# Moving the wait loop of a merge branch behind gate blocks, and the gate steps to the head of a background queue

## The chip, the cores and the metric

One core of a Trainium2 chip runs the kernel. The metric is the device time of one execution in microseconds (us). The kernel is given as three timed executions and one profiled one. TensorE is called PE, its weight loads PEld, VectorE DVE, ScalarE ACT, GpSimd POOL, SyncE SP.

## The reference

Two layers over a sequence of 512 tokens of width 1024, all in fp32. Each layer mixes three token mixers (retention, gated linear attention, softmax attention with forget gates) through gates of their own, then runs a gated feed-forward with a convolution over three tokens.

```python
def hybrid_layer(x, c_act, ...):
    mod = c_act @ w_ada + b_ada
    shift1, scale1, gate1, shift2, scale2, gate2 = jnp.split(mod, 6, axis=-1)
    h = modulate(rms_norm(x, norm1_g), shift1, scale1)
    (rq, rk, rv, rg, gq, gk, gv, glr, gg, fq, fk, fv, ff) = jnp.split(h @ w_in, split_points, axis=-1)
...
    ret = jax.nn.silu(rg) * ret          # retention of rq, rk, rv, group norm
...
    log_a = jax.nn.log_sigmoid((glr @ w_gla_a2 + b_gla_a).astype(F32)) / GLA_TAU
...
    gla_o = jax.nn.silu(gg) * gla_o      # gated linear attention of gq, gk, gv, log_a
    fox_o = forgetting_attention(rms_norm(heads(fq, FOX_D), q_norm_g),
                                 rms_norm(heads(fk, FOX_D), k_norm_g),
                                 heads(fv, FOX_D), ff + b_fox_f).reshape(b, s, BRANCH_W)
    branches = jnp.stack([ret, gla_o, fox_o], axis=2).astype(h.dtype)
    y_br = jnp.einsum('bsnw,nwd->bsnd', branches, w_br)
    gates = jax.nn.sigmoid(h @ w_mg + b_mg).reshape(b, s, N_BRANCH, D_MODEL)
    mixed = jnp.sum(gates * y_br, axis=2) @ w_o
    x = x + (gate1[:, None, :] * mixed).astype(x.dtype)
...
    u, g = jnp.split(h2 @ w_up, 2, axis=-1)
    u = causal_dwconv(u, w_conv, b_conv)
    y = (jax.nn.silu(u) * g) @ w_down
```

## The kernel before

The activations stay transposed in SBUF as 128x512 tiles (`slot`), eight for a width of 1024. A product in fp32 is three matmuls: a tile is split into a high part that ACT casts (`hi`) and a low part that DVE subtracts (`lo`), and `mm3` (L293 to L295) multiplies high by high, high by low and low by high. Weights come as units of 128x1024 from the DRAM tensor `wall`, in the order in which they are used. For each unit SP issues the transfer, ACT casts (L173, `wh`) and DVE subtracts (L182, `wl`). For the pair groups (below) POOL also issues transfers that add one unit onto another (L165).

A layer runs a foreground stream on PE: the head group, the remaining key/query blocks, a token group (`tok_group`, gla keys and the small columns of both gates, L694 to L696), two blocks `gq`, two pair groups (`pair_group`: seven products `prod` of 2 x 12 = 24 matmuls, L644 to L648; the first gives fox and gla values, the second ret values and the ret gate), the blocks `rq`, `rk`, `gg`, the merge, the output block and the feed-forward. A column block `col_block` is 24 matmuls.

Everything small runs as **background items**, Python generators on `queue`. An item is a chain of steps. A step marked "p" issues PE work, needs PSUM banks of the pool `psa` (three banks, NA) and can have conditions on earlier results; a step marked "e" issues what ACT, DVE and POOL do with it. `tick()` takes at most one item from the queue if the counter `cool` is 0 (the second number of a queue entry is the new `cool`), then advances every active item by one "e" step, evacuates the foreground blocks that are done, and advances by one "p" step. A column block ticks in the middle and at the end, a pair product once. The order of each engine is thus fixed by the ticks when the program is built; at run time each engine takes its instructions in that order.

The items that matter: `qk_norm` (eight, L541 to L561: square, cast, two matmuls `qn` with a tile of ones, then L551 to L554 on ACT), `gates_item` (transposes `smT`, L726, L731 to L733, L737 to L740 with a scan over tokens, transposes `cumc` L744, then POOL's DMAs `cumd` and `cumb` L747 and L750 which spread the sums over the partitions), `la_item` (two: `la`, `laS`, `lan`, the log-decays), `fox_item` (sixteen: scores `fs` L802, softmax, transposes `fT` L818, values `fo` L828), `kv_item` (states of gla, L871), `ret_item` (sixteen: `rs` L941, `ro` L953, then L962 to L972 for the norm), `gla_item` (`go` L919, L927 to L933), and `head_out` (L895 to L908, transposes `oT` L902, L531 and L532 for the split).

The merge runs over three branches, `order = (2, 0, 1)`: fox, ret, gla. A branch has four rounds, each of two gate blocks (gate logits of two column blocks) and 24 matmuls with the branch's result (`fb` tiles for fox, `ob` for ret and gla). Ahead of a branch's first gate block a loop ticks until the branch's last head is ready, without foreground work between the ticks. From the merge on in layer 0, every second tick also does an ada step on DVE (L203, a product of 128x1024).

Of the kernel before, what the change touches and what calls it, by code (L numbers as in the profile page):

```python
# [10 lines left out]
AF = mybir.ActivationFunctionType  # L11
# [15 lines left out]
NH = 4  # L27
HD = 128
DFF = 2816
KD = D // 128  # L30
# [20 lines left out]
NC = _o  # L51


H0 = slice(0, S // 2)
H1 = slice(S // 2, S)

# [30 lines left out]
def tile_hybrid_layers(ctx: ExitStack, tc: tile.TileContext, xT, cvec, wall, wada, par, a2, cst, tabs, out):  # L87
# [14 lines left out]
    def slot(nm, dt=F32):  # L102
        return slots.tile([128, S], dt, tag="slot", name=nm)
# [39 lines left out]
    def dbg(*a):  # L143
        if DBG:
            print(*a, tickcount[0], "unit", cur[0])
# [99 lines left out]
    queue = []  # L245
# [19 lines left out]
    def tick(n=1, fl=True):  # L265
        for g in active:
            g[2] = False
        if cool[0] > 0:
            cool[0] -= 1
        if queue and len(active) < 8 and cool[0] == 0:  # L270
            it, cool[0] = queue.pop(0)
            active.append([it, next(it), False])
        advance("e")
        if fl:
            flush()
        advance("p")
        if ada_on[0] and tickcount[0] % 2 == 1:
            ada_step()
        tickcount[0] += 1
        if DBG:  # L280
            print("T", tickcount[0], len(active), len(queue), live[0], cur[0], [g[0].__name__ for g in active])

    tickcount = [0]
    cool = [0]
# [17 lines left out]
    def ahead():  # L302
        prep_to(cur[0] + depth[0])
        dma_to(cur[0] + depth[0] + far[0], far[0] > 1)
# [230 lines left out]
    def layer(l, nm, h):  # L535
# [43 lines left out]
        A.preload_act_table_set("natural_log_exp_and_others")  # L579
        for i, o in enumerate(banks):  # L580
            qk_evac(i)(o)
        cool[0] = 8
        ahead()
        free(NA)

# [30 lines left out]
            tt[k, 1], tt[k, 2] = (ah, al, 0), (ah, al, 256)  # L616
            tt[k, 3], tt[k, 4] = (bh, bl, 0), (bh, bl, 256)

        def pair_group(done):
            flush()  # L620
            while live[0] > NA - 1:
                tick()
            q = {}
            for k in range(4):
                q[k, 11], q[k, 12] = (*h[k], 0), (*h[k], 256)
                q[k, 21], q[k, 22] = (*h[k + 4], 0), (*h[k + 4], 256)
            bA, bB = [bm(), bm()], [bm(), bm()]
            o11, o12, o21, o22 = ([slot("pr"), slot("pr")] for _ in range(4))

            def prod(banks, key, first, evac):  # L630
                us = []
                for t in range(2):
                    flush()
                    prep_lo(cur[0] + 3 - t)
                    prep_hi(cur[0] + 4 - t)
                    dma_to(cur[0] + 10, True)
                    if not t:
                        us = [unit(), unit()]
                    for k in range(4):
                        ah, al, o = q[k, key] if key > 4 else tt[k, key]  # L640
                        ts = slice(o + t * 128, o + t * 128 + 128)
                        wh, wl = us[k // 2]
                        ws = slice((k % 2) * S, (k % 2) * S + S)
                        T.matmul(banks[t], lhsT=ah[:, ts], rhs=wh[:, ws], start=first and k == 0, stop=False,  # L644
                                 skip_group_check=True)
                        T.matmul(banks[t], lhsT=ah[:, ts], rhs=wl[:, ws], start=False, stop=False,  # L646
                                 skip_group_check=True)
                        T.matmul(banks[t], lhsT=al[:, ts], rhs=wh[:, ws], start=False, stop=k == 3,  # L648
                                 skip_group_check=True)
                        if k == 1 and not t:  # L650
                            tick()
                    pend.append(lambda t=t: evac(t))

            prod(bA, 11, True, lambda t: A.copy(o11[t], bA[t]))
            prod(bB, 1, True, lambda t: A.copy(o22[t], bB[t]))
            while live[0] > NA - 1:
                tick()
            bC = [bm(), ba()]

            def e11(t):  # L660
                V.tensor_tensor(o11[t], o11[t], bC[t], op=ALU.add)
                if t:
                    free()

            prod(bC, 21, True, e11)
            prod(bA, 2, False, lambda t: A.copy(o12[t], bA[t]))
            prod(bA, 3, False, lambda t: V.scalar_tensor_tensor(out=o22[t], in0=bA[t], scalar=-1.0, in1=o22[t],
                                                                op0=ALU.mult, op1=ALU.subtract))
            prod(bB, 22, False, lambda t: V.tensor_tensor(o12[t], o12[t], bB[t], op=ALU.add))

            def e21(t):
                A.activation(o21[t], bA[t], AF.Copy, scale=-1.0)
                if t:
                    done(o11 + o12, o21 + o22)

            prod(bA, 4, False, e21)
# [27 lines left out]
        def gk_evac(b, o):  # L704
            if b == 0:
                R["gk"] = [slot("gk"), slot("gk")]
                R["sml"] = sm_p.tile([128, NB, 20], F32, tag="sml", name="sml")
            A.copy(R["gk"][b // 2][:, (b % 2) * 256:(b % 2) * 256 + 256], o[:, 0:256])
            V.tensor_copy(R["sml"][:, b, :], o[:, 256:276])  # L709
            if b == NB - 1:  # L710
                queue.append((gates_item(), 1))
                queue.append((la_item(0), 1))
                queue.append((la_item(1), 1))
                for hh in range(NH):
                    for ib in range(NB):
                        queue.append((fox_item(hh, ib), 1 + ib // 2))
# [281 lines left out]
                R["rv", b] = v[b]  # L998
                R["rg"].append(t)

        pair_group(fg_done)
        R["cos"], R["sin"] = slot("cos"), slot("sin")
        Q.dma_start(out=R["cos"], in_=tabs[0])
        Q.dma_start(out=R["sin"], in_=tabs[1])
        pair_group(r_done)
        tt.clear()
        far[0] = 1
        for i in range(4):
# [18 lines left out]
        for bi, br in enumerate(order):  # L1027
            dbg("mg", bi, br)
            if bi == 2:
# [3 lines left out]
                for _ in range(200):  # L1033
                    if not (queue or active):
                        break
                    tick()
            while ("br", br, NH - 1) not in R:
                tick()
            dbg("mg start", bi, br)
            for pr in range(KD // 2):  # L1040
                gts = {}

                def sg_evac(i, j, gts=gts):
                    def f(o):
                        g = slot("mg")
                        A.activation(g, o, AF.Tanh, scale=0.5, bias=der[l][:, i * 8 + j:i * 8 + j + 1])  # L1046
                        gts[j] = g
                    return f

                for j in (2 * pr, 2 * pr + 1):  # L1050
                    col_block(h, sg_evac(br, j))
                ahead()
                wh, wl = unit()
                for jj in range(2):
# [186 lines left out]
def _layout(inputs):  # L1241
# [17 lines left out]
    def put(tiles):  # L1259
        units.append(np.concatenate(list(tiles), axis=1))  # L1260

    for l in range(L):
# [35 lines left out]
        for br in (2, 0, 1):  # L1298
            wg = f["w_mg"][l][:, br * D:(br + 1) * D]
            wb = f["w_br"][l, br]  # L1300
            for pr in range(KD // 2):
                put(blk(wg, 2 * pr))
                put(blk(wg, 2 * pr + 1))
                put(list(blk(wb, 2 * pr)) + list(blk(wb, 2 * pr + 1)))
        cols(f["w_o"][l])
        wu = f["w_up"][l][:, :DFF]
# [93 lines left out]
```

## Time and profile before

| | before |
|---|---|
| three timed executions, median (us) | 1839.98 (1839.25 to 1844.28) |
| profiled execution (us) | 1841.36 |
| its span (us) | 1839.6 |
| PE busy (us, share of the span) | 1797.5 (98%) |
| DVE busy | 1068.0 (58%) |
| ACT busy | 724.1 (39%) |
| POOL busy | 126.4 (7%) |

The span reaches from the first instruction of the profile to the last; 1.8 us of the profiled execution lie around it. A busy share is the time in which an engine has an instruction under way. Matmuls overlap, so two of them that start 0.23 us apart are each listed with 0.4 us; the distance of the starts tells what one costs.

### The profile page before, as it was taken

The page shows a single profiled execution, that of the slowest core. Times are in us where ns is not written, and L with a number is a line of the kernel's source. Part 1 is how long each engine was busy: PE and PEld are TensorE (multiplying, and loading weights), DVE is VectorE, ACT ScalarE, POOL GpSimd, SP SyncE. Part 2 cuts the span into 40 slices and gives each one's busy share as a digit, 9 for nine tenths or more (in the row PEclk, how much of TensorE's full clock was granted, in tenths as well). Part 3 has the DMA queues.
Part 4 walks back from the last instruction along what each step waited for, and adds up shares of the span by engine and source line. Part 5 has one row for each costly group of instructions (what it writes and reads, how often), then busy time and mean ns, then how long its engine had stood idle before and what let it go on. Part 6 is the DMA issues. An engine that isn't in the chain of part 4 may idle for free.

```text
span 1839.6 us, 22717 instructions
## 1 busy us (share of the span) xinstructions
PE 1797.5 (98%) x8895; PEld 1497.6 (81%) x8895; DVE 1068.0 (58%) x1643; ACT 724.1 (39%) x1196; POOL 126.4 (7%) x152
## 2 busy tenths in 40 slices
PE   9999899999999999999999999999999999999999
PEld 6877686888889888888897777778888898888887
DVE  7867765675665776763246777644634566444321
ACT  3567442342333443332136664424323244333220
POOL 3122110010000000000001221100100000000000
PEclk9999898999999999999999999999999999999999
DMA  9487133346552465553323771312332233222131
GB/s 356 126 195 202 46 118 112 126 142 224 195 168 82 155 228 192 183 204 128 109 76 101 189 208 42 126 64 64 123 116 92 71 102 115 92 94 102 43 126 50
DMA packets 72519, 243.11 MB, mean 132 GB/s; under 512 B 8232, under 2 KB 8658, under 8 KB 72412
## 3 DMA queue, kind: packets, MB, share of 16 engines
q1 hardware_dynamic: 66444, 220.67, 35.5%
q0 software_dynamic: 5968, 20.99, 5.8%
q8 instruction: 70, 1.15, 0.3%
q14 instruction: 37, 0.30, 0.0%
HBM read 237.41 MB, written 4.21 MB: 131 GB/s over the span
## 4 chain that ended last, share of the span: by engine, by line
PE 80%; DVE 8%; ACT 4%; DMA 4%; issue 3%; POOL 1%; SPq 0%; ACTq 0%; DVEq 0%; POOLq 0%
PE bm L293 22%; PE bm L295 22%; PE bm L294 22%; PE bm L426 4%; PE ga L426 4%; DMA wr<-wall 3%; ACT wh L173 2%; DVE wl L182 2%; PE rs L941 1%; PE ro L953 1%; DVE fl L808 1%; PE bm L644 1%; PE bm L646 1%; PE bm L648 1%; DVE fst L809 1%
## 5 line engine op out<-in xcount | busy, mean ns | idle before, releaser
L182 DVE TENSOR_TENSOR wl<-wr,wh 128x1024 fp32r<-128x1024 f32 x326 | 396.9, 1222 | 301.8 <-ACT wh L173 301.6
L293 PE MATMUL bm<-hhi,wh 128*128 128x512 f32 x1232 | 500.5, 406 | 2.2 <-DVE sml L709 2.2
L295 PE MATMUL bm<-hhi,wl 128*128 128x512 f32 x1232 | 484.0, 393 | 0.0
L294 PE MATMUL bm<-hlo,wh 128*128 128x512 f32 x1232 | 483.7, 393 | 0.0
L173 ACT CAST wh<-wr 128x1024 fp32r<-128x1024 f32 x326 | 339.1, 1049 | 327.0 <-PE bm L294 201.6
L293 PEld LDWEIGHTS bm<-hhi,wh 128*128 128x128 f32 x1232 | 234.2, 190 | 56.3 <-issue 5.0
L294 PEld LDWEIGHTS bm<-hlo,wh 128*128 128x128 f32 x1232 | 233.8, 190 | 52.5 <-issue 3.7
L295 PEld LDWEIGHTS bm<-hhi,wl 128*128 128x128 f32 x1232 | 233.5, 190 | 50.2
L293 PE MATMUL bm<-fah,wh 128*128 128x512 f32 (+1 forms) x374 | 141.0, 377 | 0.0
L295 PE MATMUL bm<-fah,wl 128*128 128x512 f32 (+1 forms) x374 | 140.8, 377 | 0.0
L294 PE MATMUL bm<-fal,wh 128*128 128x512 f32 (+1 forms) x374 | 140.8, 377 | 0.0
L203 DVE SCALAR_TENSOR_TENSOR ar<-ar,cact 128x1024 f32<-128x1024 f32 x80 | 97.5, 1219 | 0.0
L1083 DVE SCALAR_TENSOR_TENSOR x<-bm,mod,x 128x512 f32<-128x512 f32 (+1 forms) x39 | 25.5, 654 | 103.1 <-PE bm L295 103.0
L295 PEld LDWEIGHTS bm<-fah,wl 128*128 128x128 f32 x374 | 70.4, 188 | 13.0
L293 PEld LDWEIGHTS bm<-fah,wh 128*128 128x128 f32 x374 | 70.4, 188 | 12.9
L294 PEld LDWEIGHTS bm<-fal,wh 128*128 128x128 f32 x374 | 70.4, 188 | 12.8
L1046 ACT ACTIVATE mg<-bm,der 128x512 f32<-128x512 f32 x48 | 33.1, 689 | 95.9 <-PE bm L295 95.9
L1120 ACT ACTIVATE fu<-fu 128x512 f32<-128x512 f32 x44 | 27.9, 635 | 103.0 <-DVE fu L1118 103.0
L1121 DVE TENSOR_TENSOR fu<-fu,bm 128x512 f32<-128x512 f32 x42 | 28.9, 688 | 64.8 <-PE bm L295 53.4
L332 ACT ACTIVATE sq<-x 128x512 f32<-128x512 f32 (+1 forms) x35 | 18.8, 547 | 104.1 <-DVE x L1083 102.9
L293 PE MATMUL bm<-mxh,wh 128*128 128x256 f32 (+1 forms) x176 | 58.6, 333 | 0.0
L295 PE MATMUL bm<-mxh,wl 128*128 128x256 f32 (+1 forms) x176 | 58.3, 331 | 0.0
(259 smaller groups left out, 2733.7 us busy)
## 6 DMA issues: line engine op xcount, KB each, us to landing
wr<-wall SPq DMA_DIRECT2D x302, 512.0 KB, 3.8
ar<-wada SPq DMA_DIRECT2D x80, 512.0 KB, 4.3
wr<-wall POOLq DMA_DIRECT2D x32, 512.0 KB, 7.7
ad<-wada SPq DMA_DIRECT2D x32, 256.0 KB, 6.1
x<-xT SPq DMA_DIRECT2D x16, 256.0 KB, 5.3
cumb<-cumd POOLq DMA_DIRECT2D x8, 256.0 KB, 5.4
dec<-tabs SPq DMA_DIRECT2D x8, 256.0 KB, 2.7
x<-xs SPq DMA_DIRECT2D x8, 256.0 KB, 5.4
```

Of the source, the lines that this page charges most:

```text
L173: A.copy(hi, raw[plan[i][1]])
L182: V.tensor_tensor(lo, raw[plan[i][1]], hi.bitcast(F32), op=ALU.subtract)
L203: V.scalar_tensor_tensor(out=r, in0=r, scalar=1.0, in1=cact, op0=ALU.mult, op1=ALU.mult, accum_out=mod[l][:, b:b + 1])
L293: T.matmul(o, lhsT=wh, rhs=ah, start=first, stop=False)
L294: T.matmul(o, lhsT=wh, rhs=al, start=False, stop=False)
L295: T.matmul(o, lhsT=wl, rhs=ah, start=False, stop=last)
L332: A.activation(t[:, ts], x[k][:, ts], AF.Square)
L426: T.matmul(banks[f % GB][:, ts], lhsT=got[f // 8][wi][:, (f % 8) * 128:(f % 8) * 128 + 128], rhs=h[kc][hi][:, ts], start=kc == 0 and hf != ...
L1046: A.activation(g, o, AF.Tanh, scale=0.5, bias=der[l][:, i * 8 + j:i * 8 + j + 1])
L1083: V.scalar_tensor_tensor(out=x[j][:, ts], in0=o[:, ts], scalar=mod[l][:, sec * 8 + j:sec * 8 + j + 1], in1=x[j][:, ts], op0=ALU.mult, op1= ...
L1120: A.activation(t, t, AF.Silu)
L1121: V.tensor_tensor(t, t, pg, op=ALU.mult)
```

## The change

Four edits. **One**: in the merge, the gate blocks are grouped by the tables MG0 (first branch: four blocks, none, two, two) and MG1 (the others: two each), and the loop that waits for the branch's last head stands behind the round's gate blocks, ahead of its product with the branch's result. The host packs the weights in the same order. **Two**: `gates_item` and the two `la_item` go to the head of the queue instead of its end, each with a `cool` of 2. **Three**: the first `cool` is 12 in layer 1, 8 in layer 0 as before. **Four**: a pair group is told how many ticks each of its seven products has; in the second pair the last three have two.

```diff
@@ -51,6 +51,8 @@
 NC = _o
 
 
+MG0 = ((0, 1, 2, 3), (), (4, 5), (6, 7))
+MG1 = ((0, 1), (2, 3), (4, 5), (6, 7))
 H0 = slice(0, S // 2)
 H1 = slice(S // 2, S)
 
@@ -579,7 +581,7 @@
         A.preload_act_table_set("natural_log_exp_and_others")
         for i, o in enumerate(banks):
             qk_evac(i)(o)
-        cool[0] = 8
+        cool[0] = 12 if l else 8
         ahead()
         free(NA)
 
@@ -616,7 +618,7 @@
             tt[k, 1], tt[k, 2] = (ah, al, 0), (ah, al, 256)
             tt[k, 3], tt[k, 4] = (bh, bl, 0), (bh, bl, 256)
 
-        def pair_group(done):
+        def pair_group(done, nts):
             flush()
             while live[0] > NA - 1:
                 tick()
@@ -629,6 +631,7 @@
 
             def prod(banks, key, first, evac):
                 us = []
+                nt = nts.pop(0)
                 for t in range(2):
                     flush()
                     prep_lo(cur[0] + 3 - t)
@@ -647,7 +650,7 @@
                                  skip_group_check=True)
                         T.matmul(banks[t], lhsT=al[:, ts], rhs=wh[:, ws], start=False, stop=k == 3,
                                  skip_group_check=True)
-                        if k == 1 and not t:
+                        if k == 1 and t < nt:
                             tick()
                     pend.append(lambda t=t: evac(t))
 
@@ -708,9 +711,7 @@
             A.copy(R["gk"][b // 2][:, (b % 2) * 256:(b % 2) * 256 + 256], o[:, 0:256])
             V.tensor_copy(R["sml"][:, b, :], o[:, 256:276])
             if b == NB - 1:
-                queue.append((gates_item(), 1))
-                queue.append((la_item(0), 1))
-                queue.append((la_item(1), 1))
+                queue[0:0] = [(gates_item(), 2), (la_item(0), 2), (la_item(1), 2)]
                 for hh in range(NH):
                     for ib in range(NB):
                         queue.append((fox_item(hh, ib), 1 + ib // 2))
@@ -998,11 +999,11 @@
                 R["rv", b] = v[b]
                 R["rg"].append(t)
 
-        pair_group(fg_done)
+        pair_group(fg_done, [1] * 7)
         R["cos"], R["sin"] = slot("cos"), slot("sin")
         Q.dma_start(out=R["cos"], in_=tabs[0])
         Q.dma_start(out=R["sin"], in_=tabs[1])
-        pair_group(r_done)
+        pair_group(r_done, [1] * 4 + [2] * 3)
         tt.clear()
         far[0] = 1
         for i in range(4):
@@ -1034,21 +1035,20 @@
                     if not (queue or active):
                         break
                     tick()
-            while ("br", br, NH - 1) not in R:
-                tick()
-            dbg("mg start", bi, br)
-            for pr in range(KD // 2):
-                gts = {}
-
-                def sg_evac(i, j, gts=gts):
-                    def f(o):
-                        g = slot("mg")
-                        A.activation(g, o, AF.Tanh, scale=0.5, bias=der[l][:, i * 8 + j:i * 8 + j + 1])
-                        gts[j] = g
-                    return f
-
-                for j in (2 * pr, 2 * pr + 1):
+            gts = {}
+
+            def sg_evac(i, j, gts=gts):
+                def f(o):
+                    g = slot("mg")
+                    A.activation(g, o, AF.Tanh, scale=0.5, bias=der[l][:, i * 8 + j:i * 8 + j + 1])
+                    gts[j] = g
+                return f
+
+            for pr, gs in enumerate(MG0 if bi == 0 else MG1):
+                for j in gs:
                     col_block(h, sg_evac(br, j))
+                while ("br", br, NH - 1) not in R:
+                    tick()
                 ahead()
                 wh, wl = unit()
                 for jj in range(2):
@@ -1298,9 +1298,9 @@
         for br in (2, 0, 1):
             wg = f["w_mg"][l][:, br * D:(br + 1) * D]
             wb = f["w_br"][l, br]
-            for pr in range(KD // 2):
-                put(blk(wg, 2 * pr))
-                put(blk(wg, 2 * pr + 1))
+            for pr, gs in enumerate(MG0 if br == 2 else MG1):
+                for j in gs:
+                    put(blk(wg, j))
                 put(list(blk(wb, 2 * pr)) + list(blk(wb, 2 * pr + 1)))
         cols(f["w_o"][l])
         wu = f["w_up"][l][:, :DFF]
```

In the changed file these lines stand one to three lower, so L533 there is L531 before, L963 is L962, L997 is L996, L903 is L902.

PE in the first merge branch of layer 0. `fo`, `fT` and `fs` are the fox steps, `kv` the gla states, `rs` the ret scores, `bm<-hhi` the gate blocks, `bm<-fbh` the products with the fox result. Before, between the last column block and the first gate block:

```order
L295 MATMUL bm<-hhi,wl 128x512
L828 MATMUL fo<-fpT,pr 128x128 x4
L818 MATMUL fT<-cst,fl 128x128 x3
L802 MATMUL fs<-qk 128x512
L828 MATMUL fo<-fpT,pr 128x128
L818 MATMUL fT<-cst,fl 128x128 x3
L828 MATMUL fo<-fpT,pr 128x128 x2
L871 MATMUL kv<-pr,lae 64x128 x8
L828 MATMUL fo<-fpT,pr 128x128 x3
L818 MATMUL fT<-cst,fl 128x128 x4
L871 MATMUL kv<-pr,lae 64x128 x8
L828 MATMUL fo<-fpT,pr 128x128 x4
```

After, the last half of the fourth gate block and the first product with the fox result:

```order
L297 MATMUL bm<-hhi,wl 128x512
L872 MATMUL kv<-pr,lae 64x128 x8
L942 MATMUL rs<-rq,rk 128x512
L295 MATMUL bm<-hhi,wh 128x512
...
L297 MATMUL bm<-hhi,wl 128x512
L942 MATMUL rs<-rq,rk 128x384
L295 MATMUL bm<-fbh,wh 128x512
```

The fox steps and the `kv` steps have moved in between half gate blocks.

ACT at the end of the second pair group of layer 0. L672 and L675 are the same evacuation of a pair product, L996 and L997 the tanh of the ret gate. Before:

```order
L672 ACTIVATE pr<-bm 128x512
L996 ACT_TABLE_LOAD
L996 ACTIVATE rg<-pr 128x512 x4
L173 CAST wh<-wr 128x1024
L770 ACTIVATE lae<-la 128x512
L771 ACTIVATE lae<-lae 128x512
L772 ACT_TABLE_LOAD
```

After:

```order
L544 ACTIVATE qsq<-qk 128x512
L675 ACTIVATE pr<-bm 128x512
L997 ACT_TABLE_LOAD
L997 ACTIVATE rg<-pr 128x512 x4
L553 ACT_TABLE_LOAD
L553 ACTIVATE qy<-qn,cst 128x512
L554 ACTIVATE qv<-qn,cst 128x512
L555 ACT_TABLE_LOAD
L555 ACTIVATE qy<-qy 128x512
L556 ACTIVATE qsq<-qy 128x512
L530 CAST qsh<-qsq 128x512
```

The log-decay steps (L770 to L772) have left this place, and steps of the key/query norm have come to it.

PE at the start of the second merge branch (ret) of layer 0. `oT` are the transposes of `head_out` (`ros` for ret, `gos` for gla), `ro` and `go` the values of ret and gla. Before, between the last product with the fox result and the first gate block:

```order
L295 MATMUL bm<-fbh,wl 128x512
L902 MATMUL oT<-cst,gos 128x128 x4
L919 MATMUL go<-st,gq 64x128 x8
L902 MATMUL oT<-cst,ros 128x128 x4
L902 MATMUL oT<-cst,gos 128x128 x4
L919 MATMUL go<-st,gq 64x128 x8
L293 MATMUL bm<-hhi,wh 128x512
```

After, between the second gate block and the first product with the ret result:

```order
L297 MATMUL bm<-hhi,wl 128x512
L903 MATMUL oT<-cst,ros 128x128 x4
L954 MATMUL ro<-pr,rP 128x128 x4
L920 MATMUL go<-st,gq 64x128 x8
L903 MATMUL oT<-cst,gos 128x128 x4
L920 MATMUL go<-st,gq 64x128 x8
L903 MATMUL oT<-cst,ros 128x128 x4
L903 MATMUL oT<-cst,gos 128x128 x4
L920 MATMUL go<-st,gq 64x128 x8
L295 MATMUL bm<-obh,wh 128x512
```

The short loop has moved behind two gate blocks, and it holds eight pieces instead of five.

## Rows read from the trace of the kernel before

**Rows 1.** The page's first section: busy time, share and instructions of each engine.

```profile
PE 1797.5 (98%) x8895; PEld 1497.6 (81%) x8895; DVE 1068.0 (58%) x1643; ACT 724.1 (39%) x1196; POOL 126.4 (7%) x152
```

**Rows 2.** Waits of PE: line, releaser, us in total, times, longest us.

```profile
PE qn L547 <- ACT qsh L528: 4.1, 1, 4.1
...
PE cumc L744 <- DVE cum L740: 3.3, 1, 3.3
PE bm L293 <- DVE sml L709: 2.2, 1, 2.2
```

**Rows 3.** Timeline of PE, layer 1, column block: start us, duration, instruction.

```profile
1191.13 0.39 PE L295 MATMUL bm<-hhi,wl 128*128 128x512 f32 x1
1191.36 0.60 PE L828 MATMUL fo<-fpT,pr 128*128 128x128 f32 x4
1191.89 0.67 PE L871 MATMUL kv<-pr,lae 64*64 64x128 f32 x16
```

**Rows 4.** Windows: length; busy PE, PEld, DVE, ACT, POOL; PE clock; DMA share; GB/s.

```profile
84.00:89.44 5.44, 5.44 (x24) 4.52 (x25) 5.06 (x13) 4.26 (x8) 0.09 (x1) 1.00 0.01 2
...
181.41:215.50 34.09, 26.99 (x104) 21.53 (x103) 22.53 (x37) 18.86 (x30) 5.67 (x7) 0.80 0.21 62
1066.38:1111.45 45.07, 41.21 (x185) 32.80 (x184) 32.25 (x46) 26.77 (x43) 5.77 (x8) 0.96 0.67 202
278.81:302.58 23.77, 19.48 (x119) 13.44 (x118) 14.48 (x33) 7.70 (x15) 0.00 (x0) 0.71 0.25 83
1195.35:1207.78 12.43, 10.62 (x81) 7.63 (x80) 7.31 (x17) 3.57 (x5) 0.00 (x0) 0.86 0.14 44
386.22:390.84 4.62, 3.67 (x46) 2.92 (x44) 3.31 (x8) 2.96 (x12) 0.85 (x1) 1.00 0.02 4
990.61:1004.26 13.65, 9.51 (x30) 7.06 (x28) 10.86 (x22) 9.01 (x18) 1.28 (x1) 0.75 0.00 0
...
996.40:1004.26 7.86, 7.86 (x26) 6.21 (x24) 5.79 (x12) 5.53 (x13) 1.28 (x1) 0.68 0.00 0
```

**Rows 5.** Timeline of ACT, layer 0, end of the second pair group.

```profile
180.63 0.57 ACT L672 ACTIVATE pr<-bm 128x512 f32<-128x512 f32 x1
181.22 1.28 ACT L996 ACT_TABLE_LOAD   x1
182.51 2.19 ACT L996 ACTIVATE rg<-pr 128x512 f32<-128x512 f32 x4
184.61 1.04 ACT L173 CAST wh<-wr 128x1024 fp32r<-128x1024 f32 x1
```

**Rows 6.** Timeline of DVE, layer 0, the forget gates ahead of `cumc`.

```profile
186.98 0.67 DVE L737 TENSOR_TENSOR fm<-fm,fe 4x512 f32<-4x512 f32 x1
...
188.33 1.21 DVE L740 TENSOR_TENSOR_SCAN cum<-fe,fm 4x512 f32<-4x512 f32 x1
```

**Rows 7.** Timeline, layer 0, last steps of ret heads; in brackets idle time and releaser.

```profile
373.39 0.69 ACT L531 ACTIVATE obh<-oT,der 128x512 fp32r<-128x512 f32 x1 [1.36 <-PE oT L902]
...
377.27 0.20 ACT L968 ACTIVATION_READ_ACCUMULATOR rsq<-ros,rst 128x1 f32 x1
...
379.18 0.69 DVE L929 COPY gos<-go 128x512 f32<-128x512 f32 x1 [2.18 <-ACT gsq L927]
379.78 1.22 DVE L203 SCALAR_TENSOR_TENSOR ar<-ar,cact 128x1024 f32<-128x1024 f32 x1
...
382.37 1.01 POOL L972 TENSOR_TENSOR rst<-rst,cst 128x4 f32<-128x4 f32 x1 [6.28 <-DVE rst L971]
...
385.55 0.29 DVE L898 TENSOR_TENSOR ros<-ros,rg 128x128 f32<-128x128 f32 x1
...
386.85 0.75 DVE L908 SCALAR_TENSOR_TENSOR gos<-oT,der,gg 128x512 f32<-128x512 f32 x1 [0.93 <-PE oT L902]
387.52 0.87 DVE L895 TENSOR_SCALAR gos<-gos,gst 128x128 f32<-128x128 f32 x4
```

**Rows 8.** Timeline of POOL, layer 0: the spread of the forget gates.

```profile
198.08 2.21 POOL L750 DMA_DIRECT2D cumb<-cumd  x4 [1.77 <-DMA cumd<-cum]
```

## The prediction

> **What bounds the kernel now.** I read the page first: TensorE (PE) is busy 1797.5 us of a span of 1839.6 [rows 1]. The time is PE's own stream plus the places where it stands still or runs at the low clock. Next came PE's waits: a `qn` of the key/query norm waits 4.1 us on ACT's cast, `cumc` of the forget gates waits 3.3 on the scan [rows 2]. Then the stretches around these waits, by windows, each against the work that is in it [rows 4].
>
> The work of a stretch I count by start-to-start distances at full clock: a 128x512 matmul takes 0.23 us (0.227 over longer runs), four `fo` pieces 0.53, sixteen `kv` pieces at most 0.67 [rows 3]. `rs`, `fs`, `la`, `laS` and `lan` pieces are smaller sums of the same kind; together they carry an error of some 0.5 us in each stretch.
>
> Six kinds of loss stand near the change:
> - Layer 1, third unit of the token group, 13.65 us: 24 full matmuls and a few small ones, 6.1. Lost 7.5, of which 4.1 is the `qn` wait [rows 2, 4].
> - Layer 0, the forget-gate and log-decay steps after the second pair, 34.09: 60 full matmuls are 13.6, the small ones 6.7, so 20.3. Lost 13.8.
> - Layer 1, end of the second pair, 45.07: 138 full ones are 31.3, small ones 6.9, so 38.2. Lost 6.9.
> - The wait loop before the first merge branch in layer 0, 23.77: 28 `fo` passes 3.1, 64 `kv` 2.7, 12 matmuls 2.7, the rest 2.3, so 10.8. Lost 13.0. In layer 1, 12.43 against 7.4. Lost 5.0.
> - The short loop before the second branch, 4.62 with 3.67 busy; 1.0 in each layer, 2.0.
>
> Sum 48.2. These are all that the change can take away; nothing else in the stream is touched. Part of it is clock, not standing: in the 13.65 the granted clock falls to 0.68 for the 24 matmuls behind the wait, which take 7.86 for 5.44 [rows 4]. A fall behind a wait is worth 2.4 there.
>
> **What the change takes away.** The loop that empties the background work before the first branch goes behind its first four gate blocks, 96 matmuls. By the order, the `fox` and `kv` steps now stand between half gate blocks, and the first `fb` matmul comes directly behind a gate block and one `rs`. So both first drains go: 18.0. The forget gates go into the token group and the first pair, the log-decay steps into the pairs. The stretch in layer 0 goes (13.8), the end of the pair in layer 1 as well (6.9), and the `qn` that stood in the token group of layer 1 goes back by four counts of `cool`, behind the gate steps: 7.5. With the short loops, all 48.2 is removed. Of the moved steps their own work (counted above as work) stays.
>
> **What it adds, step by step.**
>
> *The new gate steps.* `cumc` is issued in the same tick as L737, the memset and the scan. In the trace, L737 begins at 186.98 and the scan ends at 188.33 + 1.21: 2.6 us [rows 6]. In the new order no matmul stands between, so PE waits 2.6 to 2.8 in each layer. A fall of the clock may follow; I take half of it, 1.0 (0 to 2.4). `smT` moves up to the last evacuation of the token group, 0.4 each. Sum 8.2 for two layers (5 to 11). POOL: the DMAs of `cumd` and `cumb` now stand ahead of seven accumulating weight transfers of the pairs. `cumb` waited 1.77 for `cumd` and took 2.21 to issue [rows 8], so these transfers come about 4 us later. They are ordered six units ahead of use, three products of 24 matmuls, some 16 us; I cost this at nothing, 0 to 4 in a layer if that cover is thinner than I think. `fs` needs `cumb` later than the gates come now; on SP the weights keep their number and follow the new order of the blocks, and nothing is moved past them.
>
> *The second pair.* Three more ticks pull the `qn` steps into its last three products, and the order shows what ACT then has to do at its end. Counted from P, the end of PE's last pair matmul: the next-to-last L672 is due at P - 2.7, 12 matmuls earlier. Behind it stand a weight cast (1.04 [rows 5]), L551 to L554, a cast L528, a second weight cast, L542, and only then the last L672. From one start to the next a 512-wide instruction like L672 takes 0.59 (180.63 to 181.22) [rows 5]; I take 0.6 for each. So ACT finishes the last L672 at P + 4.25. Behind it: a table load (1.28), four L996 (2.1), a load, L551 and L552 (1.15), a load, L553 and L554 (1.2), the cast that the last `qn` needs (0.6): P + 13.2. Before, one load and four L996 stood there and nothing of `qn` behind. PE has 12 matmuls, `qn` #7, 24 matmuls, and is at `qn` #8 at P + 9.3. It waits 3.9, with #7 some 5.5 (3 to 7). Such a wait was followed by the low clock above: 2.4. Handovers to `fs` behind it 0.6. Sum 8.5 in each layer, 17 (10 to 22).
>
> What a load costs is read here: the load at 181.22 starts 0.02 after L672 ends, and the next ACTIVATE at 182.51, 0.01 after the load's 1.28 [rows 5]. The Trainium skill, ScalarE: Activation LUTs, section "What ACT_TABLE_LOAD costs", gives about 1283 ns for the load and 1380 ns of drain with it, 2.66 us for a switch. The trace agrees with the first and shows none of the second. By the page, three loads would put `qn` #8 off by 4.1 more in each layer; that is a rival below.
>
> *The fox steps between gate blocks.* Their waits on ACT and DVE are covered by 12 matmuls (2.7 us) each; 1 us in a layer for what sticks out, 2 together (0 to 6).
>
> *The second branch.* Here the change does not do what it says. It doesn't remove a drain, it moves one. Before, the loop ahead of the first branch also advanced the `ret` and `gla` steps; now these are further back, and after two gate blocks the order has, without one full matmul between: `oT`, `ro`, `go`, `oT`, `go`, `oT`, `oT`, `go`, then the first `ob` matmul. The chain of the last `ret` head, from the trace of the same steps [rows 7]: `oT` and on ACT L531 up to the fourth L968, 373.39 to 377.47, is 0.55 + 4.1; L927 till DVE's copy L929, 377.47 to 379.18, 1.7 (the new order also has L927 ahead, and L929 waits on it); L929 0.69; L971 0.3; POOL's power and the eight scalings, 382.37 to 385.84, 3.5. That is 10.8. Behind the scalings DVE has L932, an ada step (1.22 and 0.08, layer 0 alone), L908 0.75, L895 0.87, L929 0.69, before the last `go` gets its bank: 14.5. The `go` itself takes 1.0. So 15.5 in layer 0 and 14.2 in layer 1. Work in it: five pieces like 0.53 and three `go`, 5.75. Lost 9.75 and 8.45, 18.2; in both drains of before the granted clock was low, 0.71 and 0.86 over the stretch [rows 4]; I add 2 each, a little under the 2.4 above. Together 22 (16 to 26). The third branch is emptied in both kernels by a loop of its own.
>
> *More table loads, longer cool.* The longer `cool` in layer 1 makes the order of both layers alike; the extra loads are priced where they stand. The rest I cost at nothing, since it only changes which tick of a pair a step falls on; bounds 0 to 3 for the end of layer 1's pair.
>
> **The sum.** 8.2 + 17 + 2 + 22 = 49.2 new against 48.2 taken: +1. The profiled execution took 1841.4, 1.4 above the median; +1 on the median of 1840.0 gives **1841**. What this measurement can tell from no change is 0.3%, 5.5 us.
>
> **Rivals.**
> - *The clock doesn't fall at the new waits* (chance 0.20). For it: `bm` waited 2.2 on `sml` [rows 2] and the clock behind it, from 84.00 on, was 1.00 [rows 4]; the `cumc` waits are near that. Against: in the stretches of the waits of 3.3 and 4.1 it was 0.80 and 0.75. Then 2 x 2.4 for `qn`, 4 for the drains, 2 for `cumc` are not paid: 10.8 less, 1830.
> - *The `qn` at the end of the pair comes in time* (0.16). My chain has ACT 4.25 late at P. If its weight casts run ahead instead, L672 ends some 3 earlier, the wait of 3.9 shrinks to 1 and the fall behind it goes: 2 x (2.9 + 2.4) less, 1830.
> - *Slower: ACT never catches up behind the pair* (0.17). Place: the `fs` and `fT` steps in the column blocks between pair and merge; each needs an exponential on ACT, which now starts them 4 us late, with two loads more in the queue. It decides when the lag at `qn` #8 is over the two ticks (5.4) that a step has: then six steps in each layer wait about 0.8: 2 x 5 more, 1851.
> - *Loads as the page has them* (0.05): 2 x 4.1 more, 1849. A mechanism of this kernel: three loads stand ahead of the cast of `qn` #8. The row at 181.22 speaks against it.
> - *Forecast* (0.42): 1835 to 1846, no change that can be told.
>
> **How the numbers follow.** Faster by over 0.3%: the first two rivals, 0.36. Slower: the next two, 0.22. Same: 0.42. The range takes in the rivals' own times and leaves out some tenth on each side: 1828 to 1851.
>
> **What would show it.** In the trace of the changed kernel: no gap over 1 us between the first four gate blocks and `fb`; `cumc` waits 2.6 twice; PE waits 3 to 6 on the last two `qn` of each layer, behind three loads on ACT; between the second gate block and the first `ob` 14 to 16 us. I'm wrong if that last stretch is under 8 us (then faster, by about 15), or if pair products wait for weights that POOL accumulates (then slower).

## The result and the profile after

| | before | after |
|---|---|---|
| median of six executions each (us) | 1839.26 (1830.73 to 1844.28) | 1847.28 (1846.28 to 1848.98) |
| profiled execution, its span (us) | 1841.36, 1839.6 | 1847.60, 1845.8 |
| ratio, 95% interval | | 1.0052 [1.0028, 1.0076] |

The changed kernel is 0.5% slower, 8 us by the medians and 6.2 by the two spans. The page's first section of after stands against [rows 1]: PE has the same number of instructions, and its busy time is the same within 1.1 us, so the loss is time in which PE stands. ACT has four instructions more, all of them table loads.

```profile
PE 1796.4 (97%) x8895; PEld 1493.8 (81%) x8895; DVE 1067.9 (58%) x1643; ACT 727.9 (39%) x1200; POOL 125.7 (7%) x152
```

PE's waits after, as in [rows 2] (line, releaser, us in total, times, longest):

```profile
PE qn L549 <- ACT qsh L530: 7.6, 2, 3.8
PE oT L903 <- DVE gos L896: 6.6, 4, 2.1
PE oT L903 <- DVE ros L899: 5.4, 2, 3.0
PE fs L803 <- ACT fpT L822: 4.1, 4, 1.1
PE cumc L745 <- DVE cum L741: 4.1, 2, 2.1
PE qn L550 <- DVE qsl L531: 3.1, 8, 0.9
```

Nearly all of these come twice, once in a layer: both layers now run the same order. The long waits are the last `qn`, the `oT` transposes of the ret branch, `cumc`, and the fox scores `fs`.

Where the loss sits is told by a table. For each stretch it gives the time that PE took over what its instructions need when they follow each other at full clock: the stretch's length, less a price for each instruction by its kind. The prices are fitted to all places of the fourteen traces where PE neither waits nor has a lower clock. A stretch with no wait and full clock comes out at 0.7 or less, such as the fox branches after. "Up to the pairs" is the token group, `gq` and both pair groups, "blocks" are the column blocks `rq`, `rk` and `gg`.

| us lost | before | after | forecast of the difference | measured |
|---|---|---|---|---|
| layer 0, up to the pairs | 8.7 | 9.6 | +4.1 | +0.9 |
| layer 0, blocks | 14.5 | 14.4 | -5.3 | -0.2 |
| layer 0, fox branch | 12.6 | 0.7 | -12.0 | -11.9 |
| layer 0, ret branch | 1.1 | 12.3 | +10.8 | +11.2 |
| layer 1, up to the pairs | 16.2 | 7.4 | -10.3 | -8.9 |
| layer 1, blocks | 4.9 | 14.4 | +8.5 | +9.6 |
| layer 1, fox branch | 5.1 | 0.7 | -4.0 | -4.4 |
| layer 1, ret branch | 1.1 | 11.0 | +9.5 | +9.9 |

The forecast's column is the sum of the prediction, its terms put into the stretches (a fall of the clock goes with its wait, the fox steps between gate blocks go to the fox branch). It adds up to +1.2, the measured one to +6.2, which is the difference of the spans.

### The profile page after: what moved, and what is told of

It is laid out like the page before. It is cut to its first block, busy times and chain, and to the rows that moved or that the text cites. A ratio compares the mean times of both kernels' runs of the same rounds, so it can differ in the third digit from the quotient of the medians.

```text
span 1845.8 us, 22722 instructions
## 1 busy us (share of the span) xinstructions
PE 1796.4 (97%) x8895; PEld 1493.8 (81%) x8895; DVE 1067.9 (58%) x1643; ACT 727.9 (39%) x1200; POOL 125.7 (7%) x152
## 4 chain that ended last, share of the span: by engine, by line
PE 83%; DVE 8%; ACT 5%; issue 2%; DMA 1%; POOL 0%; SPq 0%; ACTq 0%; DVEq 0%; POOLq 0%
PE bm L295 22%; PE bm L297 22%; PE bm L296 21%; PE bm L428 4%; PE ga L428 4%; ACT wh L175 2%; DVE wl L184 2%; PE bm L649 2%; PE bm L647 2%; PE bm L651 2%; PE rs L942 1%; PE ro L954 1%; DVE fl L809 1%; DMA wr<-wall 1%; DVE rt L841 1%
## 5 line engine op out<-in xcount | busy, mean ns | idle before, releaser
L334 ACT ACTIVATE sq<-x 128x512 f32<-128x512 f32 (+1 forms) x35 | 18.8, 545 | 103.9 <-DVE x L1083 102.9
L296 PE MATMUL bm<-mxl,wh 128*128 128x256 f32 (+1 forms) x176 | 58.3, 331 | 0.0
```

Source lines behind the costliest of these rows:

```text
L296: T.matmul(o, lhsT=wh, rhs=al, start=False, stop=False)
```

## The experiments

Every comparison is with the kernel before on the same chip, whose medians in the three groups were 1838.7 (e1, e2, e3, e5), 1840.7 (e9 to e12) and 1839.4 (e6, e14, e16c, e16). In an experiment's file a line can stand a few lower or higher than in the changed one.

### Which edit costs: the merge alone, the rest alone

The first edit undone, the other three kept:

```diff
-            for pr, gs in enumerate(MG0 if bi == 0 else MG1):
-                for j in gs:
+            while ("br", br, NH - 1) not in R:
+                tick()
+            for pr in range(KD // 2):
+                for j in (2 * pr, 2 * pr + 1):
                     col_block(h, sg_evac(br, j))
-                while ("br", br, NH - 1) not in R:
-                    tick()
```

> The changed kernel with its first edit undone (blocks of the merge and wait loops as before; gate steps at the head of the queue, cool of 12 and the added ticks stay). Theory (the ret drain behind two gate blocks costs 13 us a layer, the first drain 14): the ret drain goes, 26 less, but the first drain comes back in both layers, since the order of PE there is that of layer 0 before in both, 27 more: 1849, no better than the changed kernel. Rival (the first edit is the whole slowing and the other three bring something): under 1839, some 1831.

Measured: 1847.74, ratio 1.0046 [1.0029, 1.0063]. The first drain is back in both layers (10.2 and 9.7 us lost in the fox branches) and the ret branch loses 1.1 each, as before. Both moves are smaller than the theory had them, some 19 and 21 for 27 and 26, and nearly cancel.

The kernel before with the first edit alone:

```diff
+            for pr, gs in enumerate(MG0 if bi == 0 else MG1):
+                for j in gs:
+                    col_block(h, sg_evac(br, j))
+                while ("br", br, NH - 1) not in R:
+                    tick()
```

> The kernel before with the first edit alone (blocks and wait loops of the merge). Theory: the first drains go in both layers (14 and 7), the ret drain comes in layer 0 alone (13), because in layer 1 the order shows each ret step between halves of a block: 1839 - 21 + 13 - 1 = 1830. Rival (the first edit is the whole slowing): 1847.

Measured: 1836.56, 0.9981 [0.9969, 0.9992]. The sign is the theory's, the gain a quarter of what it gave. In the profiled execution the fox branches lost 0.6 each and the ret branches 12.6 and 0.3, in the places that were expected, but the first drains were worth 16.4 and not 21. That execution was 2.9 above its own median and lost 19.1 up to the pairs of layer 1, where the kernel before lost 16.2 with the same order of PE, so some of the rest is spread between executions. What follows: neither half alone is the cause. The first edit without the rest brings a little, the rest without the first costs 0.5%.

### The ret drain: cover it

Four gate blocks first in the ret branch too:

```diff
-            for pr, gs in enumerate(MG0 if bi == 0 else MG1):
+            for pr, gs in enumerate(MG0 if bi < 2 else MG1):
```

> The changed kernel with four gate blocks first in the ret branch too (the table MG0 for the first two branches). Theory: each step of the ret drain then stands between 12 matmuls (2.7 us), and the drain's 13 us go in each layer: 1847 - 26 = 1821, up to 1827 where waits of a step stick out of 2.7 us. Rival (the chain of a ret head on ACT, DVE and POOL is longer than the cover and the stall only moves): 1840 or more, with PE waits on ros and gos of over 2 us in the new place.

Measured: 1824.46, 0.9923 [0.9907, 0.9938]. The same eight pieces of the ret drain, on PE's timeline (start us, duration, instruction, idle and releaser in brackets). The changed kernel, where they follow each other:

```profile
383.54 0.60 PE L903 MATMUL oT<-cst,ros 128*128 128x128 f32 x4
383.98 1.06 PE L954 MATMUL ro<-pr,rP 128*128 128x128 f32 x8
384.96 1.09 PE L920 MATMUL go<-st,gq 64*64 64x128 f32 x16
388.18 0.82 PE L903 MATMUL oT<-cst,gos 128*128 128x128 f32 x4 [2.13 <-DVE gos L896]
388.94 1.09 PE L920 MATMUL go<-st,gq 64*64 64x128 f32 x16
392.44 2.13 PE L903 MATMUL oT<-cst,ros 128*128 128x128 f32 x4 [2.42 <-DVE ros L899]
396.59 1.09 PE L903 MATMUL oT<-cst,gos 128*128 128x128 f32 x4 [2.01 <-DVE gos L896]
397.68 1.97 PE L920 MATMUL go<-st,gq 64*64 64x128 f32 x16
```

With four blocks first (the matmuls of the gate blocks between them are left out):

```profile
382.25 0.60 PE L903 MATMUL oT<-cst,ros 128*128 128x128 f32 x4
382.68 1.06 PE L954 MATMUL ro<-pr,rP 128*128 128x128 f32 x8
...
386.44 1.09 PE L920 MATMUL go<-st,gq 64*64 64x128 f32 x16
...
393.08 0.60 PE L903 MATMUL oT<-cst,gos 128*128 128x128 f32 x4
393.61 1.09 PE L920 MATMUL go<-st,gq 64*64 64x128 f32 x16
...
397.53 0.60 PE L903 MATMUL oT<-cst,ros 128*128 128x128 f32 x4
```

No wait in brackets is left, and the transposes take 0.60 instead of up to 2.13. The whole ret branch holds the same instructions of PE in both kernels. Its windows (length; busy PE, PEld, DVE, ACT, POOL; clock; DMA share; GB/s), layer 0 and layer 1 of the changed kernel, then the same with four blocks first:

```profile
367.34:457.27 89.93, 83.11 (x415) 67.62 (x414) 59.65 (x113) 32.24 (x93) 8.57 (x6) 0.92 0.49 164
1280.11:1368.75 88.64, 82.96 (x416) 67.50 (x414) 44.91 (x86) 31.81 (x93) 6.89 (x6) 0.92 0.29 95
```

```profile
366.04:444.14 78.10, 78.10 (x416) 64.45 (x414) 57.03 (x109) 31.87 (x93) 9.40 (x6) 1.00 0.52 175
1267.66:1345.76 78.10, 78.10 (x416) 64.44 (x415) 44.84 (x86) 31.80 (x93) 7.12 (x6) 1.00 0.33 108
```

PE is busy all of it at a granted clock of 1.00 with four blocks first, and the branch is 11.8 and 10.5 us shorter, which together is the 22.8 between the medians but for 0.5. The work of ACT, DVE and POOL is nearly the same; the pieces now stand later on PE, behind other matmuls.

The opposite: the loop of the ret and gla branches ahead of their first gate block, as before the change, the fox branch as changed.

```diff
+            while bi and ("br", br, NH - 1) not in R:
+                tick()
             for pr, gs in enumerate(MG0 if bi == 0 else MG1):
```

> The changed kernel with the wait loop of the ret and gla branches ahead of their first gate block, as before; the fox branch stays as changed. Theory (what counts is how many blocks with ticks lie between the ret steps and the loop): the loop now has four ticks more of ret steps without cover, at 1 to 1.5 us each: 4 to 6 more in each layer, 1855 to 1859. Rival (the loop's new place, behind the evacuations of two gate blocks, makes the drain long): the drain shrinks to the 4.6 us of before, 1827 to 1832.

Measured: 1859.68, 1.0109 [1.0094, 1.0125]. The ret branches lose 18.8 and 15.7 for 12.3 and 11.0. So the loop's place behind two blocks is no cost; it is worth 12 us against the old place. It is short of cover, not badly placed.

The first edit alone, with four blocks first in the ret branch (the diff of e2 and that of e3 on the kernel before):

> The kernel before with the first edit alone and four gate blocks first in the ret branch too. Theory (the stalls of both drains are what the whole change moves; the gate steps, the cool and the ticks bring nothing): the kernel with the first edit alone at 1836.6 loses its ret drain of 13 us in layer 0: 1823 to 1825, the time of the changed kernel with four ret blocks. Rival (the other three edits are needed for the gain): 1830 or more.

Measured: 1824.06, 0.9914 [0.9899, 0.9930]. This is the time of e3, which has the other three edits on top. Once both drains are covered, the gate steps at the head of the queue, the `cool` of 12 and the added ticks bring nothing that these runs can tell. In layer 1 they move a loss: e12 loses 14.6 up to the pairs and 5.0 in the blocks, e3 8.1 and 14.4. In layer 0 the two differ by less than 0.5 in each.

### The end of the second pair

ACT's timeline at that place in the changed kernel, layer 0; the first matmul of `rq` starts at 181.94:

```profile
185.18 0.58 ACT L675 ACTIVATE pr<-bm 128x512 f32<-128x512 f32 x1
185.77 1.28 ACT L997 ACT_TABLE_LOAD   x1
187.07 2.19 ACT L997 ACTIVATE rg<-pr 128x512 f32<-128x512 f32 x4
189.28 1.28 ACT L553 ACT_TABLE_LOAD   x1
190.58 0.69 ACT L553 ACTIVATE qy<-qn,cst 128x512 f32<-128x512 f32 x1
191.16 0.68 ACT L554 ACTIVATE qv<-qn,cst 128x512 f32<-128x512 f32 x1
191.86 1.28 ACT L555 ACT_TABLE_LOAD   x1
193.15 0.63 ACT L555 ACTIVATE qy<-qy 128x512 f32<-128x512 f32 x1
...
194.35 0.60 ACT L530 CAST qsh<-qsq 128x512 fp32r<-128x512 f32 x1
```

The last L675 ends 3.8 behind the pair, the cast that the last `qn` waits for at 194.95, 13.0 behind it, and PE goes on at 195.00 after 3.78 of waiting.

One preload of the table that holds logarithm and exponential, behind the tanh:

```diff
                 R["rg"].append(t)
+            A.preload_act_table_set("natural_log_exp_and_others")
```

> The changed kernel with one preload of the activation table that holds both the logarithm and the exponential, behind the tanh of the ret gate: between that tanh and the last qn one load instead of two, and two loads fewer behind it in each layer. Theory (loads on ACT delay the last qn and the fox steps behind it): the wait of 3.8 on the last qn falls to 2.5, the fox waits between pair and merge (5 us in layer 0, 3 in layer 1 more than before) shrink by half: 6 less, 1841. Rival (loads are hidden, the fox waits come from the order of the steps alone): 1846 to 1847.

Measured: 1844.99, 1.0033 [1.0021, 1.0046]; 2.3 less by the medians, a third of what was expected. The wait on the last `qn` is 2.4 for 3.8, as expected, and by the table's count the end of the pair (the last two `qn` and the low clock behind them) costs 4.4 in each layer for 7.2 and 7.9. But the fox steps in the blocks behind it cost 8.8 and 8.7 for 7.2 and 6.6: the waits of `fs` on `fpT` stay at 4.1 in all, and `fT` waits 2.9 on ACT where it waited 0.3. With fewer loads the fox steps wait more, so they were not late because of the loads.

The four tanh of the ret gate moved into the four `gg` blocks:

```diff
         for i in range(4):
+            pend.append(lambda i=i: rg_step(i))
             col_block(h, gate_evac("gg", i))
```

> The changed kernel with the four tanh of the ret gate moved from the end of the second pair into the four gg blocks (no table load and no tanh between the last two qn; 7 loads in all for 15). Theory (the tanh and its loads are the whole of the wait on the last qn and of the low clock behind it): the wait of 3.8 goes, 5 to 6 less in a layer: 1835 to 1838. Rival (the fox steps behind wait instead, as with the preload): 1842 to 1845.

Measured: 1840.56, 1.0000 [0.9990, 1.0009]. The wait on the last `qn` is gone, table loads fall from 15 to 7, and with them 6.7 us. It is between the two expectations. What is not gained has become waits of the fox steps on ACT:

```profile
PE fs L803 <- ACT fpT L822: 6.6, 4, 2.3
...
PE fT L819 <- ACT fpT L822: 2.5, 2, 1.3
```

4.1 became 6.6 on the first line. By the table's count the end of the pair costs 0.3 in each layer for 7.2 and 7.9, and the fox steps behind it 11.2 and 9.7 for 7.2 and 6.6: of 14.5 us, 7 are taken back. In layer 0, 1.3 of it is the last wait of `fs`, 2.3 for 1.1, which stands behind a moved tanh and its load; the waits ahead of them are no shorter than in the changed kernel. This kernel, with the ret drain in it, is level with the kernel before.

The preload with four ret blocks:

> The changed kernel with four gate blocks first in the ret branch and the table preload behind the tanh of the ret gate. Theory (the two effects stand in different places and add): 1824.5 - 2.3 = 1822. Rival (the time that the preload brings is taken back by the next wait): 1824 to 1825.

Measured: 1823.54, 0.9914 [0.9899, 0.9930]. The ratio of e3 is 0.9923 [0.9907, 0.9938], so the two can't be told apart, and neither can the expectations.

The added ticks undone, with four ret blocks:

```diff
-        pair_group(r_done, [1] * 4 + [2] * 3)
+        pair_group(r_done, [1] * 7)
```

> The changed kernel with four gate blocks first in the ret branch and the fourth edit undone (one tick in each product of the second pair). Theory (the added ticks pile ACT's work on the end of the pair): the wait of 3.8 on the last qn and the low clock behind it go, 7 less in a layer, but three kv steps stand without cover ahead of the fox product, 4 more in a layer, and four table loads more: 1819 to 1824. Rival (the ticks are what keeps the first drain away): over 1830.

Measured: 1824.50, 0.9917 [0.9901, 0.9932], just above the theory's range and the time of e3. The blocks lose 10.5 and 10.3 instead of 14.4 each, the fox branches 2.5 for 0.7 and the ret branches 4.2 and 1.8 for 0.4. The ticks are no gain: what they give in the merge they take at the end of the pair.

### The fox waits: ACT or DVE

The copies of the transposed weights out of PSUM on DVE, with four ret blocks:

```diff
-            A.copy(pT[:, 0:w], pt[:, 0:w])
+            V.tensor_copy(pT[:, 0:w], pt[:, 0:w])
```

> The changed kernel with four gate blocks first in the ret branch, and the fox copies fpT out of PSUM done by DVE instead of ACT. Theory (fs and fT wait for ACT, whose queue holds the weight cast ahead of the copy that frees the bank): the waits of fs and fT on fpT, 5.5 us in this kernel, fall to under 2: 1821. Rival (DVE, which has the low weight parts, is as late): fs waits on DVE instead, 1824 or more.

Measured: 1833.72, 0.9969 [0.9959, 0.9979], 9 more than e3. PE's waits there:

```profile
PE fs L803 <- DVE fbl L531: 5.7, 4, 1.4
PE fT L819 <- DVE fpT L822: 4.2, 2, 2.1
...
PE fs L803 <- DVE fpT L822: 3.2, 4, 1.5
```

The waits moved to DVE and nearly doubled, and the blocks lose 18.0 each for 14.4. The rival stands: DVE is as late as ACT. But DVE is the busier of the two (58% against 39%), so this run does not tell what an engine with less to do would bring. The fox steps have three banks of PSUM and one tick of 12 matmuls between steps; that this sets the waits is likely, and not shown.

### The forget gates: one tick later

The wait of `cumc`, by one more step ahead of it, with four ret blocks and the preload:

```diff
             V.tensor_tensor_scan(cum[0:4], e[0:4], m[0:4], 0.0, op0=ALU.mult, op1=ALU.add)
+            yield E_
             yield P1
```

> The changed kernel with four gate blocks first in the ret branch, the table preload, and one more step between the scan of the forget gates and its transposes, so that cumc comes one tick (24 matmuls) later. Theory (cumc waits 2.1 because it stands in the same tick as its scan): 2.1 and the low clock behind it go, 3 less in a layer: 1823.5 - 6 = 1817.5. Rival (clock unchanged, the later cumc collides elsewhere): 1820 to 1823.

Measured: 1831.21, 0.9957 [0.9943, 0.9970], 8 more than e10, where 6 less was expected. The wait of `cumc` is gone. POOL's timeline (L748 and L749 are `cumd`, L751 and L752 `cumb`, L167 the accumulating weight transfers) shows what came for it. The changed kernel:

```profile
95.37 0.56 POOL L748 DMA_DIRECT2D cumd<-cum  x1 [5.23 <-DVE cum L741]
97.44 2.19 POOL L751 DMA_DIRECT2D cumb<-cumd  x4 [1.51 <-DMA cumd<-cum]
99.61 2.75 POOL L167 DMA_DIRECT2D wr<-wall  x3
```

One tick later:

```profile
98.53 2.63 POOL L167 DMA_DIRECT2D wr<-wall  x3 [8.51 <-ACT pr L657]
100.14 1.58 POOL L749 DMA_DIRECT2D cumd<-cum  x1
112.89 2.19 POOL L752 DMA_DIRECT2D cumb<-cumd  x4 [11.18 <-DMA cumd<-cum]
115.06 1.86 POOL L167 DMA_DIRECT2D wr<-wall  x2
```

`cumd`, 8 KB, is issued behind three weight transfers of 512 KB, and `cumb` waits 11.18 for it instead of 1.51. Two weight transfers stand behind `cumb` in POOL's queue. ACT's cast then waits 10.5 for its unit (the row after its last instruction in front, at 114.10), and PE waits 12.8 in four places for the evacuations behind that cast:

```profile
125.18 1.04 ACT L175 CAST wh<-wr 128x1024 fp32r<-128x1024 f32 x1 [10.50 <-DMA wr<-wall]
```

The same step with the tanh in the `gg` blocks instead of the preload:

> Four gate blocks first in the ret branch, cumc one tick later, and the tanh of the ret gate in the gg blocks instead of the preload, all on the changed kernel. Theory: 1817.5 less what is left of the wait on the last qn (2.4 and the clock, 4 in a layer): 1809 to 1811. Rival (fox waits take it back): 1815 or more.

Measured: 1827.17, 0.9936 [0.9922, 0.9950]. It carries the same loss on POOL (13.4 and 11.3 us up to the pairs; e10 has 9.7 and 7.4) and so says little on the tanh: 4.0 below e14. Four ret blocks with the late tanh and without the added step were not tried.

## Why the prediction was right or wrong

The time fell into the range (1828 to 1851), 6 above the forecast of 1841. By the median that is slower by more than 0.3%, the side that had a chance of 0.22. By the table, 6.2 measured stand against 1.2 summed. Both drains, the last `qn` and `cumc` came as the prediction had them, nearly at its prices. What the sum left out is a wait in another place, the fox steps in the column blocks. The total is nearer than its parts, and that is luck: the blocks came out 6.2 worse than summed in the two layers, layer 0 up to the pairs 3.2 better.

**The first drains.** 16.0 forecast (18.0, less 2 for the fox steps between gate blocks), 16.3 measured, in both layers where it was put. No wait of PE stands in the fox branches after: each takes 87.81 us, with PE busy all of it at a granted clock of 1.00.

**The ret drain.** That the change moves a drain was right, its place too, and the length of the stretch nearly so. Windows of the changed kernel (length; busy PE, PEld, DVE, ACT, POOL; clock; DMA share; GB/s), first the two drains, then the 24 `ob` matmuls behind each:

```profile
383.54:399.58 16.04, 9.22 (x73) 6.54 (x71) 11.27 (x32) 8.47 (x37) 5.17 (x4) 0.72 0.25 85
1296.31:1311.22 14.91, 9.23 (x73) 6.54 (x71) 9.08 (x28) 8.15 (x37) 3.49 (x4) 0.69 0.00 1
399.58:407.34 7.76, 7.76 (x27) 6.22 (x25) 6.79 (x14) 2.73 (x11) 2.39 (x2) 0.70 0.62 204
1311.22:1318.83 7.61, 7.61 (x27) 6.10 (x25) 5.84 (x12) 2.62 (x11) 2.38 (x2) 0.71 0.43 138
```

16.0 and 14.9 against 15.5 and 14.2 forecast. Behind them 24 matmuls take 7.76 and 7.61 for 5.44, 2.3 and 2.2 of low clock, against 2 each. By the table the branch loses 11.2 and 9.9 more than before, and the sum had 10.8 and 9.5. e3, which has the same instructions there without a wait, gives the drain and its clock another way: 11.8 and 10.5, where the prediction had 11.75 and 10.45. So the term was right in mechanism, place and size. e3 and e6 bear it out from both sides: with cover the drain goes, and with less cover there are 12 us more.

**The end of the second pair.** PE waits 3.78 and 0.90 on the last `qn` in layer 0, and 0.21 on #7: 4.9, against 3.9 and 5.5 with #7. ACT's chain ended 13.0 behind the pair, 13.2 was worked out. The clock behind it was 0.90 over 10.5 us in layer 0, about 1 us, and 0.75 over 10.4 in layer 1, about 2.6; 2.4 was put in. With all of it the end of the pair cost 7.2 and 7.9 for 8.5 each: right as a wait, a little large as a price. e16c takes it away and gains only 6.7 in both layers, because the fox steps behind then wait more.

The windows behind the waits: `cumc` in layer 0 and layer 1, then the last `qn` in layer 0 and layer 1.

```profile
95.20:105.00 9.80, 9.80 (x44) 7.69 (x45) 6.05 (x9) 5.22 (x8) 5.49 (x8) 1.00 0.56 142
1007.66:1018.00 10.34, 10.34 (x40) 7.89 (x41) 6.04 (x9) 4.13 (x7) 5.45 (x8) 0.83 0.51 131
197.28:207.74 10.46, 10.46 (x43) 8.28 (x43) 8.74 (x15) 5.61 (x9) 2.58 (x2) 0.90 0.27 81
1109.10:1119.50 10.40, 10.38 (x35) 8.30 (x36) 8.71 (x12) 6.07 (x9) 2.59 (x2) 0.75 0.16 54
```

**The fox steps, the main miss.** The sum had 2 us for them between the gate blocks, and there they wait for nothing. They wait in the column blocks between pair and merge, which the sum put at nothing and only the "slower" rival had. The waits of `fs` and `fT` come to 8.2 after (4.1, 2.0, 1.8 and 0.3 in the list of waits). Before, the blocks had 2.5 of them (layer 0, then layer 1):

```profile
PE fs L802 <- ACT fpT L821: 0.6, 1, 0.6
```

```profile
PE fs L802 <- ACT fpT L821: 1.7, 2, 1.0
...
PE fs L802 <- DVE fl L806: 0.2, 1, 0.2
```

With the short stops around each wait the fox steps in the blocks cost 7.2 and 6.6 after, about 1.8 and 4.9 before (0.6 of it the log-decay's): 7.1 more in the two layers, most of it in layer 0. That is the miss of 6.2 and more; the end of the pair, 1.9 below its price, makes up for a part. This is the "slower" rival's place, but not its mechanism: the steps do wait about 1 us each as it said, yet neither the loads (e5) nor ACT's lag at the end of the pair (e16c, where the lag is gone and the waits are no shorter) set them. What sets them between a step's three banks and its one tick was argued from e9, not shown; the cause stays open.

**The gates.** `cumc` waited 2.1 twice, 2.6 to 2.8 were forecast. The clock behind it was 1.00 in layer 0 and 0.83 in layer 1 (first two windows above); half a fall was put in. The stretch of layer 0 came out 3.2 better. Most of that is from waits of pair products on DVE's low weight parts, which the kernel before has there and the list after has not; the sum left them out:

```profile
PE bm L646 <- DVE wl L182: 2.4, 3, 1.0
```

Layer 1's stretch came out 1.4 worse, which is not traced to a wait.

**POOL.** The price of 0 for `cumd` and `cumb` ahead of the weights held: no pair product waits for POOL after. e14 shows how near the edge that is. The bound of 4 in a layer, for a thinner cover, was too low: one tick later PE waits 12.8 for it in the two layers.

**The other rivals.** The clock fell behind the drains and the last `qn`, and in one layer behind `cumc`, so the first did not come. The last `qn` did not come in time. The loads as the page has them did not come either: three loads on ACT's timeline above have 1.28 each and the next instruction starts 0.01 or 0.02 after each. The Trainium skill, ScalarE: Activation LUTs, section "What ACT_TABLE_LOAD costs", counts a drain of about 1380 ns with each load; none of the three shows it, ahead of the load or behind it.

## What to carry to other kernels

A wait loop that is moved behind covered work is only half of an edit: list what the loop used to push ahead besides its own branch, because that work arrives late at the next loop. Price each of the background steps where the new order puts it: here those in blocks that the edits do not touch were the main miss. Here four blocks of cover at both branches (e12, no other edit) gain 0.9%, where the change as it was made loses 0.5%. When a background chain is pulled to another place, count its DMAs in their queue too: a small transfer behind large ones can hold everything that was queued after it.

## What the runs showed of the hardware that was not expected

- POOL waited 1.51 us for a transfer of 8 KB when POOL's last transfer ahead of it had been issued 6 us earlier, and 11.18 when three accumulating transfers of 512 KB had been issued just ahead of it (waits of `cumb` above).
- The same wait of 2.07 us on `cumc` was followed by a granted clock of 1.00 in layer 0 and 0.83 in layer 1 of one execution. The length of the wait alone does not tell whether the clock falls.
